# Values and gates of two heads, and the first merge branch, loaded in rows of 512 columns with halves that take turns

## The chip, the cores and the metric

One core of one Trainium2 chip runs the whole program: TensorE (PE, with its weight loads as PEld), VectorE (DVE), ScalarE (ACT), GpSimd (POOL), and SyncE (SP), which issues nearly all DMAs. The metric is the time of one execution on the device in microseconds; lower is better.

## The reference, cut to what matters

One layer of a hybrid decoder runs over 288 tokens (256 of a prompt, 8 samples of 4). All weights are read once, so the kernel is a long stream of matmuls against weights that pass through.

```python
D_MODEL = 2048; RET_HEADS = GLA_HEADS = 4; DV = 256; GDN_HEADS = 8
h = rmsnorm(x, norm_mix)
(rq, rk, rv, rg, dqkv, da, db, dz, lq, lk, lv, llr, lgt, mg) = split(h @ w_in)   # 16416 columns
y_ret = rmsnorm(retention(rq, rk, rv)) * silu(rg)             # 4 heads, value width 256
y_gdn = rmsnorm(gated_delta(conv(dqkv), ...)) * silu(dz)      # 8 heads
y_gla = rmsnorm(gla(lq, lk, lv, ...)) * silu(lgt)             # 4 heads, value width 256
gates = sigmoid(mg + b_merge)                                  # 3 branches x 2048 columns
x = x + (sum_i gates_i * (y_i @ w_branch[i])) @ w_o
x = x + (silu(hn @ w_gate) * (hn @ w_up)) @ w_down             # hn = rmsnorm(x)
```

## The kernel before

Every product is computed transposed: a block of 128 weight columns is the stationary operand, and the 288 tokens stream past it. Weights and activations are fp32. Each is split into a rounded part and a rest (`wh` and `wl`, `xh` and `xl`), and three matmuls (wh·xh, wh·xl, wl·xh) make one product of a 128 x 128 block. SP loads a weight piece `raw` of 512 KB, ACT casts it to `wh` (128 x 512 elements), DVE subtracts to get `wl`, PE multiplies. There are four buffers each of `raw`, `wh` and `wl`, and one `wh` with its `wl` feeds 12 matmuls.

The work comes in two shapes of load. In the mixers and in merge branch 0, `dense` and `products` (L361 to L401) take 256 columns: a `raw` is four k-tiles (4 x 128 rows of the weight) of 256 columns, so each row of it is 1 KB. I call a product of 256 columns over all 16 k-tiles a unit; it is four raws and 96 matmuls, and it accumulates in two of the four PSUM banks `pd`. In merge branches 1 and 2, the output projection and the feed-forward part, `wide` and `products4` (L326 to L359) take 512 columns: a `raw` is two k-tiles of 512 columns, 2 KB a row. These accumulate in four banks, turn by turn in `pd` and in `pm`.

The mixers run in the order gdn 0, ret 0, gdn 1, ret 1, gdn 2, gla 0, gdn 3, gla 1. A gdn pair has four units (q, k, v, gate). A ret or gla pair has six: q, k, and then value and gate of its first head, value and gate of its second. The mixing itself (scores, states, norms, on `pm`) is written as generators. `pump` (L158) advances them a step after each k-tile of a unit: one step for gdn mixing, then one for all other kinds. So mixing of one pair lies between the matmuls of the next units. A ret or gla head starts after its gate unit, as `ret_head` (L1084) or `gla_head` (L1157), and both end in `wide_head` (L943).

The gdn mixing inverts 8 x 8 blocks on DVE, and it moves them by way of DRAM: `bt` is written to `dgb` and `dgbs` (L684, L685), read back as `b8` (L688), solved in `u8` (L692 to L704), written to `dgu` and `dgus` (L706), and read as `uc` (L709). All these DMAs are issued on SP in one queue with the raws. L692 is the copy that sets `u8` up for the next gdn pair; it must wait until the writes out of the old `u8` have landed.

Merge branch 0 (`branch`, L1256) is eight times a gate unit (`mg`, 16 k-tiles) and a product with `w_branch` (8 k-tiles), both in 256 columns, while the last gla heads are still mixed. The order on each engine is made by the framework's scheduler, in which the weight loads, casts and subtractions have high priority.

Of the kernel before, what the change touches and what calls it, by code (L numbers as in the profile page):

```python
# [10 lines left out]
F32 = mybir.dt.float32  # L11
F32R = mybir.dt.float32r
I32 = mybir.dt.int32
AF = mybir.ActivationFunctionType
ALU = mybir.AluOpType
# [3 lines left out]
P = 128  # L19
# [5 lines left out]
T = NPR + NS  # L25
KT = D // P
# [4 lines left out]
WIDE = 512  # L31
CHUNK = 256
# [9 lines left out]
EV = 9  # L42

O_RQ, O_RK, O_RV, O_RG = 0, 512, 1024, 2048
O_GQ, O_GK, O_GV = 3072, 4096, 5120
O_DA, O_DZ = 6144, 6160
O_LQ, O_LK, O_LV, O_LLR, O_LG = 7184, 7696, 8208, 9232, 9248
O_MG = 10272
# [47 lines left out]
def blocks(t):  # L96
    return [t[:, k] for k in range(t.shape[1])]


class Trunk:  # L100
# [225 lines left out]
    def wide(self, xh, xl, wv, kt, evict):  # L326
# [5 lines left out]
            evict(m, tiles[m][:, :T])  # L332
        return pool

    def products4(self, xh, xl, wv, kt, steps=None):
        nc, tc = self.nc, self.tc
        pool, tag = ((self.pd, "pd"), (self.pm, "pm"))[self.turn]
        self.turn = 1 - self.turn
        acc = [self.t(pool, (P, 512), tag) for _ in range(4)]
        for k0 in range(0, kt, 2):  # L340
            raw = self.t(self.wp, (P, 2, WIDE), "raw", bufs=4)
            with tc.high_priority():
                nc.sync.dma_start(out=raw, in_=wv[:, k0:k0 + 2])
            for k in range(2):
                wh = self.t(self.wp, (P, WIDE), "wh", F32R, bufs=4)
                wl = self.t(self.wp, (P, WIDE), "wl", F32R, bufs=4)
                with tc.high_priority():
                    nc.scalar.copy(wh, raw[:, k])  # L348
                    self.tt(wl, raw[:, k], wh.bitcast(F32), ALU.subtract)
                kk = k0 + k  # L350
                for m in range(4):
                    ms = slice(m * P, (m + 1) * P)
                    o = acc[m][:, :T]
                    self.mm(o, wh[:, ms], xh[kk], kk == 0, False)
                    self.mm(o, wh[:, ms], xl[kk], False, False)
                    self.mm(o, wl[:, ms], xh[kk], False, kk == kt - 1)
            if steps is not None:
                next(steps)
        return (pool, tag), acc  # L359
# [208 lines left out]
    def gated(self, n, c0):  # L568

        out = self.t(self.mx, (P, 2, T), "ev", bufs=EV)  # L570

        def ev(m, pp):
            th = self.r1()
            self.tt(out[:, m], pp, self.rb, ALU.mult)
            self.act(th, out[:, m], AF.Tanh, scale=0.5)
            self.stt(out[:, m], th, 1.0, out[:, m], ALU.add, ALU.mult)

        self.x_in(c0, ev)
        return out

    def finish(self, tr_ps, gate, gcol, n, blk):

# [360 lines left out]
    def wide_head(self, h, st, st2, vt, vs, zq, kd, s0, state_out, p_out, decay, sg, gcols, n):  # L943


        nc, m = self.nc, self.wd
# [52 lines left out]
            nc.sync.dma_start(out=dst, in_=src)  # L999
        yield  # L1000
        yield
        for e in range(2):
            pt = self.ps()
            for g, (t0, w) in enumerate(GROUPS):
                self.tr(pt[:, t0:t0 + w], ys[g][:, e * P:(e + 1) * P])
            self.finish(pt, sg[:, e], None if gcols is None else gcols[:, e:e + 1], n, 2 * h + e)
        yield
        k3 = self.stack_k(kd[:NS, 2])
        v3 = self.stack_v(vs)
# [3 lines left out]
        for z in range(2):  # L1013
            for y in range(2):
# [5 lines left out]
                for b2 in range(2):  # L1020
                    b = 2 * y + b2
# [109 lines left out]
    def ret(self, pair):  # L1131
        q = self.rotated(O_RQ + pair * CHUNK)
        k = self.rotated(O_RK + pair * CHUNK)
        for hh in range(2):
            h = 2 * pair + hh
            v = self.evict_scaled(O_RV + h * 256)
            sg = self.gated(2, O_RG + h * 256)
            self.start(self.ret_head(h, q[:, hh], k[:, hh], v, sg), 1, "ret")


    def gla_logits(self, pair):
# [97 lines left out]
    def gla(self, pair):  # L1239
        b = self.t(self.mx, (P, 2, T), "ev", bufs=EV)  # L1240
        self.nc.sync.dma_start(out=b, in_=self.fsum[pair])
        q = self.t(self.mx, (P, 2, T), "ev", bufs=EV)

        def evq(m, pp):
            self.stt(q[:, m], pp, DK ** -0.5, self.rb, ALU.mult, ALU.mult)

        self.x_in(O_LQ + pair * CHUNK, evq)
        k = self.evict_scaled(O_LK + pair * CHUNK)
        for hh in range(2):
            h = 2 * pair + hh  # L1250
            v = self.evict_scaled(O_LV + h * 256)
            sg = self.gated(2, O_LG + h * 256)
            self.start(self.gla_head(h, q[:, hh], k[:, hh], v, sg, b[:, hh]), 1, "gla")


    def branch(self, n, order, emit=None):  # L1256
        nc = self.nc
        wb = self.i["w_branch"][0, n].rearrange("(k p) c -> p k c", p=P)
        yh, yl = [], []
        for k in range(8):  # L1260
# [4 lines left out]
            self.split(h, l, yr)  # L1265
            yh.append(h)
            yl.append(l)
        W = WIDE if n else CHUNK
        for j in range(D // W):
            th = [self.t(self.bp, (P, T), "bt", bufs=8) for _ in range(W // P)]  # L1270

            def evg(m, pp):
                blk = n * KT + W // P * j + m
                self.tt(th[m], pp, self.rb, ALU.mult)
                self.act(th[m], th[m], AF.Tanh, scale=0.5, bias=self.hbm[:, blk:blk + 1])

            if n:
                self.wide(blocks(self.xh), blocks(self.xl), self.w_in(O_MG + n * D + j * W, W), KT, evg)
            else:
                self.x_in(O_MG + j * W, evg)  # L1280

            def evb(m, pp):
                k = W // P * j + m
# [8 lines left out]
                    self.tt(self.acc[k], self.acc[k], th[m], ALU.add)  # L1292
                    emit(k, self.acc[k])

            (self.wide if n else self.dense)(yh, yl, wb[:, :, j * W:(j + 1) * W], 8, evb)

    def accs(self):
        return [self.t(self.ap, (P, T), "acc", bufs=KT) for _ in range(KT)]
# [193 lines left out]
```

## Time and profile before

| | |
|---|---|
| median of 3 runs | 2325.01 us (2323.74 to 2328.38) |
| profiled execution | 2326.31 us, of which the span from first to last instruction is 2324.2 us |
| granted TensorE clock, mean | 0.966 |
| PE busy | 2193.6 us (94%) |
| DVE busy, ACT busy | 1350.2 us (58%), 1027.2 us (44%) |
| DMA queue of SP | 366.22 MB, 64.4% of 16 engines' span |

The span falls into mixers (to about 866 us), merge branch 0 (866 to 1056 us) and the rest in rows of 512 columns. A busy share near 100% does not say that PE runs at its best, since a matmul's record is longer than the distance to the next one. Idle time, granted clock and matmuls per stretch say more. The granted clock is a share of 2.4 GHz and takes two levels, 1.0 and 0.5 (1.2 GHz); a value between is a mean over a stretch.

### The profile page before, as it was taken

What the parts mean: (1) busy time and instruction counts of PE and PEld (TensorE: products, weight loads), DVE (VectorE), ACT (ScalarE), POOL (GpSimd) and SP (SyncE); (2) the same over time, 40 slices, a digit from 0 to 9 for tenths busy, and PEclk for the clock granted to TensorE, in tenths of its full rate; (3) what the DMA queues carried; (4) which work ended last, traced back from release to release, by engine and by line L of the source; (5) the groups of instructions that cost most, each with busy time, mean ns of one, the idle gap of its engine ahead of it and who ended that gap; (6) DMA issues with size and microseconds to landing.
All of it is one profiled execution on the core that took longest, in us unless ns stands there. A gap on an engine that the chain in (4) does not pass through costs nothing.

```text
span 2324.2 us, 42820 instructions
## 1 busy us (share of the span) xinstructions
PE 2193.6 (94%) x16476; PEld 2131.1 (92%) x16476; DVE 1350.2 (58%) x2940; ACT 1027.2 (44%) x2114; POOL 209.5 (9%) x264
## 2 busy tenths in 40 slices
PE   8686998998699899999999999999999999999997
PEld 7686898988599898899999999999999999999997
DVE  4564676675378667455555655555555445555554
ACT  4352454454246445344444444444444334444443
POOL 2000230141024214100000000000000000000000
PEclk8897999998799999999999999999999999999999
DMA  8977576588766677877666656655555555555553
GB/s 172 110 113 116 138 179 148 122 185 137 108 149 158 160 127 190 175 188 203 174 180 181 166 173 193 181 167 164 166 169 165 165 167 169 164 165 168 167 157 121
DMA packets 287128, 371.73 MB, mean 160 GB/s; under 512 B 26242, under 2 KB 184028, under 8 KB 286764
## 3 DMA queue, kind: packets, MB, share of 16 engines
q1 hardware_dynamic: 285756, 366.22, 64.4%
q8 instruction: 129, 2.11, 0.4%
q0 software_dynamic: 896, 2.45, 0.3%
q14 instruction: 75, 0.61, 0.1%
q10 hardware_dynamic: 272, 0.34, 0.1%
HBM read 342.02 MB, written 26.92 MB: 159 GB/s over the span
## 4 chain that ended last, share of the span: by engine, by line
PE 80%; DMA 13%; DVE 3%; SPq 1%; ACT 1%; issue 1%; POOL 0%; POOLq 0%; DVEq 0%; ACTq 0%
PE pd L127 49%; PE pm L127 30%; DMA raw<-in_w_in_dram 5%; DMA dgu<-u 1%; PE pm L124 1%; DMA dgb<-bt 1%; DMA srow<-in_state_gdn_conv_dram 1%; DMA yr<-ys 1%; DVE wl L133 1%; DMA s<-in_state_ret_dram 1%; DMA out_dram<-s 1%; DMA uc<-dgu 1%; DMA b<-dgbs 1%; DMA ev<-fsum 0%; SPq L706 0%
## 5 line engine op out<-in xcount | busy, mean ns | idle before, releaser
L133 DVE TENSOR_TENSOR wl<-raw,wh 128x512 fp32r<-128x512 f32 (+1 forms) x1208 | 847.3, 705 | 738.8 <-ACT wh L348 490.9
L127 PE MATMUL pd<-xh,wh 128*128 128x288 f32 x2768 | 838.1, 304 | 37.5 <-ACT wh L384 33.1
L127 PE MATMUL pd<-xh,wl 128*128 128x288 f32 x2768 | 832.0, 304 | 34.0 <-DVE wl L133 33.9
L127 PE MATMUL pd<-xl,wh 128*128 128x288 f32 x2768 | 836.2, 303 | 0.2 <-DVE xl L142 0.2
L348 ACT CAST wh<-raw 128x512 fp32r<-128x512 f32 x784 | 485.0, 620 | 644.1 <-PE pd L127 331.7
L127 PEld LDWEIGHTS pd<-xh,wh 128*128 128x128 f32 x2768 | 535.0, 194 | 46.1 <-ACT wh L384 36.5
L127 PEld LDWEIGHTS pd<-xh,wl 128*128 128x128 f32 x2768 | 532.4, 194 | 42.1 <-DVE wl L133 38.5
L127 PEld LDWEIGHTS pd<-xl,wh 128*128 128x128 f32 x2768 | 535.6, 194 | 3.9 <-issue 1.0
L384 ACT CAST wh<-raw 128x512 fp32r<-128x512 f32 x416 | 254.6, 619 | 362.3 <-PE pd L127 234.8
L127 PE MATMUL pm<-xh,wl 128*128 128x288 f32 x704 | 207.8, 295 | 0.0
L127 PE MATMUL pm<-xl,wh 128*128 128x288 f32 x704 | 207.3, 294 | 0.0
L127 PE MATMUL pm<-xh,wh 128*128 128x288 f32 x704 | 207.0, 294 | 0.0
L127 PEld LDWEIGHTS pm<-xh,wl 128*128 128x128 f32 x704 | 132.1, 188 | 0.0
L127 PEld LDWEIGHTS pm<-xh,wh 128*128 128x128 f32 x704 | 132.1, 188 | 0.0
L127 PEld LDWEIGHTS pm<-xl,wh 128*128 128x128 f32 x704 | 132.0, 188 | 0.0
L127 PE MATMUL pd<-ah,wl 128*128 128x288 f32 x352 | 103.9, 295 | 0.0
L127 PE MATMUL pm<-ah,wl 128*128 128x288 f32 x352 | 103.9, 295 | 0.0
L127 PE MATMUL pm<-al,wh 128*128 128x288 f32 x352 | 103.8, 295 | 0.0
L127 PE MATMUL pd<-al,wh 128*128 128x288 f32 x352 | 103.7, 295 | 0.0
L127 PE MATMUL pm<-ah,wh 128*128 128x288 f32 x352 | 103.7, 295 | 0.0
L127 PE MATMUL pd<-ah,wh 128*128 128x288 f32 x352 | 103.6, 294 | 0.0
L147 POOL TENSOR_TENSOR fr<-fs,c_mh 128x3 f32<-128x3 f32 x1 | 0.8, 850 | 836.8 <-DVE fs L139 836.8
(367 smaller groups left out, 2894.8 us busy)
## 6 DMA issues: line engine op xcount, KB each, us to landing
raw<-in_w_in_dram SPq DMA_DIRECT2D x252, 512.0 KB
raw<-in_w_gate_up_dram SPq DMA_DIRECT2D x176, 512.0 KB
raw<-in_w_down_dram SPq DMA_DIRECT2D x88, 512.0 KB
raw<-in_w_branch_dram SPq DMA_DIRECT2D x48, 512.0 KB
raw<-in_w_o_dram SPq DMA_DIRECT2D x32, 512.0 KB
out_dram<-s SPq DMA_DIRECT2D x16, 512.0 KB
s<-in_state_gdn_dram SPq DMA_DIRECT2D x8, 512.0 KB
s<-in_state_ret_dram SPq DMA_DIRECT2D x16, 256.0 KB
```

The costliest lines, as they stand in the source:

```text
L124: self.nc.tensor.transpose(out, in_, self.ident[:k, :k])
L127: self.nc.tensor.matmul(out, lhsT=lhsT, rhs=rhs, start=start, stop=stop)
L133: self.nc.vector.tensor_tensor(out, a, b, op=op)
L147: self.nc.gpsimd.tensor_tensor(out, in_, c[:n].to_broadcast(list(in_.shape)), op=ALU.pow)
L348: nc.scalar.copy(wh, raw[:, k])
L384: nc.scalar.copy(h, src)
```

## The change

`halves` is a new product routine. It loads 512 columns in rows of 2 KB, as `wide` does: two raws of two k-tiles each, both needed for a group of four k-tiles. It then works through the group's left 256 columns and after that through its right 256, so that the halves take turns by four k-tiles. The left half accumulates in two `pd` banks and the right half in the other two, and the left half is evicted while the right one finishes. It pumps as `products` does.

`two_heads` uses it for ret and gla: one call for the values of both heads of a pair, then one for both gates. Head 0 starts after the values (before: after its value and its gate, the same number of units) and waits for its gate only near its end (`while not sg`). Head 1 starts after the gates. Merge branch 0 uses `halves` for gates and products, four times in 512 columns in place of eight times in 256. Units of gdn, and q and k of ret and gla, stay as they are.

```diff
+    def halves(self, xh, xl, wv, kt, evict):
+        acc = [self.t(self.pd, (P, 512), "pd") for _ in range(4)]
+        for k0 in range(0, kt, 4):
+            raws = []
+            for z in (k0, k0 + 2):
+                raw = self.t(self.wp, (P, 2, WIDE), "raw", bufs=4)
+                with tc.high_priority():
+                    nc.sync.dma_start(out=raw, in_=wv[:, z:z + 2])
+                raws.append(raw)
+            for half in range(2):
+                for z, raw in enumerate(raws):
+                    wh = self.t(self.wp, (P, 2, CHUNK), "wh", F32R, bufs=4)
+                    wl = self.t(self.wp, (P, 2, CHUNK), "wl", F32R, bufs=4)
+                    src = raw[:, :, half * CHUNK:(half + 1) * CHUNK]
+                    with tc.high_priority():
+                        nc.scalar.copy(wh, src)
+                        self.tt(wl, src, wh.bitcast(F32), ALU.subtract)
+                    for k in range(2):
+                        kk = k0 + 2 * z + k
...
+                        self.pump(k)
+                if k0 + 4 == kt:
+                    for m in range(2):
+                        evict(2 * half + m, acc[2 * half + m][:, :T])
...
+    def two_heads(self, cv, cg, head, kind):
+        vs = [self.t(self.mx, (P, 2, T), "ev", bufs=EV) for _ in range(2)]
...
+        self.x_halves(cv, evv)
+        gates = []
+        self.start(head(0, vs[0], gates), 1, kind)
+        gs = [self.t(self.mx, (P, 2, T), "ev", bufs=EV) for _ in range(2)]
...
+        self.x_halves(cg, evg)
+        gates.extend(gs)
+        self.start(head(1, vs[1], gates), 1, kind)
...
+        while not sg:
+            yield
...
-        for hh in range(2):
-            h = 2 * pair + hh
-            v = self.evict_scaled(O_RV + h * 256)
-            sg = self.gated(2, O_RG + h * 256)
-            self.start(self.ret_head(h, q[:, hh], k[:, hh], v, sg), 1, "ret")
+        self.two_heads(O_RV + pair * WIDE, O_RG + pair * WIDE,
+                       lambda hh, v, sg: self.ret_head(2 * pair + hh, q[:, hh], k[:, hh], v, sg), "ret")
...
-        W = WIDE if n else CHUNK
+        W = WIDE
...
-                self.x_in(O_MG + j * W, evg)
+                self.x_halves(O_MG + j * W, evg)
...
-            (self.wide if n else self.dense)(yh, yl, wb[:, :, j * W:(j + 1) * W], 8, evb)
+            (self.wide if n else self.halves)(yh, yl, wb[:, :, j * W:(j + 1) * W], 8, evb)
```

SP's queue, where ret 0 goes over from its k unit to the values, before. The rows from L684 on are the gdn mixing's way through DRAM.

```order
L323 DMA raw_328_1615<-in_w_in_dram 128x4x256
L323 DMA raw_348_1688<-in_w_in_dram 128x4x256
L1146 DMA r2_333_1635<-in_gla_w_up_dram 16x256
L1146 DMA r2_340_1664<-in_gla_w_up_dram 16x256
L323 DMA raw_366_1764<-in_w_in_dram 128x4x256
L323 DMA raw_371_1802<-in_w_in_dram 128x4x256
L684 DMA dgb_94_473<-bt4_282_1400 128x512
L685 DMA dgbs_95_474<-bt2_283_1401 32x64
L323 DMA raw_376_1836<-in_w_in_dram 128x4x256
L688 DMA b8_319_1551<-dgb_94_473 16x8x8 x4
L323 DMA raw_384_1876<-in_w_in_dram 128x4x256
L688 DMA b8_319_1551<-dgbs_95_474 4x8x8 x2
```

The same place in the changed kernel:

```order
L323 DMA raw_328_1615<-in_w_in_dram 128x4x256
L345 DMA raw_351_1691<-in_w_in_dram 128x2x512
L1204 DMA r2_333_1635<-in_gla_w_up_dram 16x256
L1204 DMA r2_340_1664<-in_gla_w_up_dram 16x256
L345 DMA raw_352_1693<-in_w_in_dram 128x2x512
L345 DMA raw_374_1805<-in_w_in_dram 128x2x512
L743 DMA dgb_94_473<-bt4_282_1400 128x512
L744 DMA dgbs_95_474<-bt2_283_1401 32x64
L345 DMA raw_375_1807<-in_w_in_dram 128x2x512
L747 DMA b8_319_1551<-dgb_94_473 16x8x8 x4
L747 DMA b8_319_1551<-dgbs_95_474 4x8x8 x2
L345 DMA raw_384_1874<-in_w_in_dram 128x2x512
```

From the fifth raw on, loads of 128x4x256 have become 128x2x512, the same bytes in half as many rows. The small DMAs keep their places, except that both reads of `dgbs` now stand ahead of the next raw.

DVE's queue a little later, at the end of ret 0's k unit, before. `r1<-pd` and `ev<-pd` evict the k unit's two banks, and `u8<-b8` waits for the reads on SP above:

```order
L133 TENSOR_TENSOR wl_365_1745<-raw_348_1688,wh_364_1744 128x512
L139 TENSOR_SCALAR ev_331_1633<-pm_335_1641,cols_85_441 128x288
L133 TENSOR_TENSOR wl_368_1767<-raw_366_1764,wh_367_1766 128x512
L133 TENSOR_TENSOR r1_343_1675<-pd_300_1469,rot_240_1191 64x288 x2
L133 TENSOR_TENSOR r1_344_1680<-pd_301_1470,rot_240_1191 64x288 x2
L693 COPY u8_320_1552<-b8_319_1551 72x4
L133 TENSOR_TENSOR wl_370_1787<-raw_366_1764,wh_369_1786 128x512
```

The same place in the changed kernel:

```order
L133 TENSOR_TENSOR wl_369_1750<-raw_352_1693,wh_368_1749 128x512
L139 TENSOR_SCALAR ev_331_1633<-pm_335_1641,cols_85_441 128x288
L133 TENSOR_TENSOR wl_371_1770<-raw_351_1691,wh_370_1769 128x512
L752 COPY u8_320_1552<-b8_319_1551 72x4
L133 TENSOR_TENSOR r1_343_1675<-pd_300_1469,rot_240_1191 64x288 x2
L133 TENSOR_TENSOR r1_344_1680<-pd_301_1470,rot_240_1191 64x288 x2
L133 TENSOR_TENSOR pr2_355_1707<-b8_319_1551,u8_320_1552 72x8
L133 TENSOR_TENSOR wl_373_1790<-raw_352_1693,wh_372_1789 128x512
```

The copy `u8<-b8` stands after the same number of `wl` subtractions, but now ahead of the evictions of the k unit, and the second `wl` already needs the second raw.

## Rows read from the trace of the kernel before

**Rows 1.** The page, part 2: the span in 40 slices of 58 us
```profile
PE   8686998998699899999999999999999999999997
...
PEclk8897999998799999999999999999999999999999
DMA  8977576588766677877666656655555555555553
```

**Rows 2.** Stretches, a late one: engines' busy us (instructions), granted clock, DMA share, GB/s
```profile
1300.00:1350.00 50.00, 50.00 (x380) 50.00 (x379) 27.73 (x50) 23.38 (x41) 0.00 (x0) 1.00 0.55 168
```

**Rows 3.** Stretches: ret 0 in two, ret 1's and gla's values and gates
```profile
134.00:184.00 50.00, 38.48 (x263) 34.43 (x262) 29.20 (x99) 26.27 (x68) 3.04 (x2) 0.93 0.74 114
184.00:261.00 77.00, 64.67 (x580) 60.85 (x579) 37.47 (x89) 24.01 (x51) 2.88 (x6) 0.87 0.65 118
...
384.00:454.50 70.50, 67.33 (x624) 63.60 (x623) 38.43 (x98) 26.54 (x61) 7.19 (x10) 0.98 0.59 123
...
577.00:673.00 96.00, 74.40 (x648) 69.67 (x647) 46.47 (x136) 28.06 (x66) 16.11 (x23) 0.86 0.65 110
...
788.00:866.00 78.00, 71.75 (x648) 66.68 (x647) 45.03 (x129) 28.13 (x64) 15.96 (x23) 0.98 0.69 122
```

**Rows 4.** Waits by engine, 168 to 184 us: in total, times, longest
```profile
DVE u L693 <- DMA b<-dgbs: 13.0, 1, 13.0
...
PE pd L127 <- DVE wl L133: 9.3, 1, 9.3
```

**Rows 5.** Waits by engine, 200 to 216 us
```profile
DVE u L692 <- DMA dgu<-u: 14.7, 1, 14.7
...
PE pd L127 <- DVE wl L133: 9.9, 1, 9.9
...
PE pd L127 <- ACT wh L384: 2.0, 1, 2.0
```

**Rows 6.** Waits by engine, 575 to 616 us
```profile
DVE u L693 <- DMA b<-dgbs: 13.5, 1, 13.5
...
PE pm L127 <- DVE tmc L718: 10.1, 1, 10.1
...
PE pd L127 <- DVE wl L133: 9.5, 1, 9.5
DVE u L692 <- DMA dgu<-u: 9.8, 1, 9.8
```

**Rows 7.** SP in order of time, 158 to 176 us: start, us until issued, line, DMA
```profile
160.72 0.34 SPq L684 DMA_DIRECT2D dgb<-bt  x1
...
172.67 1.75 SPq L688 DMA_DIRECT2D b<-dgb  x4
```

**Rows 8.** Stretches: while raws of 1 KB rows are loaded
```profile
216.00:234.00 18.00, 17.61 (x214) 16.59 (x214) 9.65 (x22) 6.33 (x10) 0.57 (x2) 0.84 0.53 130
...
566.00:578.00 12.00, 12.00 (x95) 11.84 (x94) 7.97 (x27) 4.29 (x10) 0.00 (x0) 1.00 0.99 88
```

**Rows 9.** DMA packets from 566 to 578 us
```profile
DMA packets 1046, 1.05 MB, mean 88 GB/s; under 512 B 32, under 2 KB 1045, under 8 KB 1045
```

**Rows 10.** Stretches: while raws of 2 KB rows are loaded (branch 1)
```profile
1121.00:1139.00 18.00, 18.00 (x138) 18.00 (x138) 11.06 (x20) 6.83 (x11) 0.00 (x0) 1.00 0.73 182
1158.00:1176.00 18.00, 18.00 (x138) 18.00 (x137) 10.76 (x20) 7.60 (x14) 0.00 (x0) 1.00 0.61 178
```

**Rows 11.** DVE in order of time, 168 to 184 us: the copy, [idle before it <- what ended that]
```profile
181.90 0.17 DVE L693 COPY u<-b 72x4 f32<-72x4 f32 x1 [12.97 <-DMA b<-dgbs]
```

**Rows 12.** PE's waits, 966 to 992 us; then the stretch
```profile
PE pd L127 <- ACT wh L384: 4.1, 2, 2.4
...
972.00:992.00 20.00, 15.54 (x89) 14.60 (x88) 7.92 (x14) 5.65 (x11) 0.00 (x0) 0.83 0.96 174
```

**Rows 13.** DVE in order of time, 364 to 386 us: an eviction of the k unit
```profile
366.74 0.92 DVE L133 TENSOR_TENSOR r<-pd,rot 64x288 f32<-64x288 f32 x2
...
369.92 0.46 DVE L133 TENSOR_TENSOR ev<-pd,rot 128x288 f32<-128x288 f32 x1
```

More of the change, by code (lines that the diff above doesn't have):

```diff
@@ L333, in wide, with x_halves @@
         return pool
+    def halves(self, xh, xl, wv, kt, evict):
+        nc, tc = self.nc, self.tc
+        acc = [self.t(self.pd, (P, 512), "pd") for _ in range(4)]
[17 more added lines that the diff above has]
+                        for m in range(2):
+                            ms = slice(m * P, (m + 1) * P)
+                            o = acc[2 * half + m][:, :T]
+                            self.mm(o, wh[:, k, ms], xh[kk], kk == 0, False)
+                            self.mm(o, wh[:, k, ms], xl[kk], False, False)
+                            self.mm(o, wl[:, k, ms], xh[kk], False, kk == kt - 1)
+                        self.pump(k)
+                if k0 + 4 == kt:
+                    for m in range(2):
+                        evict(2 * half + m, acc[2 * half + m][:, :T])
+    def x_halves(self, c0, evict):
+        self.halves(blocks(self.xh), blocks(self.xl), self.w_in(c0, WIDE), KT, evict)
     def products4(self, xh, xl, wv, kt, steps=None):
@@ L579, in gated, with evv, evg @@
         return out
+    def two_heads(self, cv, cg, head, kind):
+        vs = [self.t(self.mx, (P, 2, T), "ev", bufs=EV) for _ in range(2)]
+        def evv(m, pp):
+            self.tt(vs[m // 2][:, m % 2], pp, self.rb, ALU.mult)
+        self.x_halves(cv, evv)
+        gates = []
+        self.start(head(0, vs[0], gates), 1, kind)
+        gs = [self.t(self.mx, (P, 2, T), "ev", bufs=EV) for _ in range(2)]
+        def evg(m, pp):
+            out = gs[m // 2][:, m % 2]
+            th = self.r1()
+            self.tt(out, pp, self.rb, ALU.mult)
+            self.act(th, out, AF.Tanh, scale=0.5)
+            self.stt(out, th, 1.0, out, ALU.add, ALU.mult)
+        self.x_halves(cg, evg)
+        gates.extend(gs)
+        self.start(head(1, vs[1], gates), 1, kind)
     def finish(self, tr_ps, gate, gcol, n, blk):
@@ L1005, in wide_head @@
                 self.tr(pt[:, t0:t0 + w], ys[g][:, e * P:(e + 1) * P])
-            self.finish(pt, sg[:, e], None if gcols is None else gcols[:, e:e + 1], n, 2 * h + e)
+            self.finish(pt, sg[h % 2][:, e], None if gcols is None else gcols[:, e:e + 1], n, 2 * h + e)
         yield
@@ L1248, in gla @@
         k = self.evict_scaled(O_LK + pair * CHUNK)
[L1249 to L1253, printed above, removed]
+        self.two_heads(O_LV + pair * WIDE, O_LG + pair * WIDE,
+                       lambda hh, v, sg: self.gla_head(2 * pair + hh, q[:, hh], k[:, hh], v, sg, b[:, hh]), "gla")
     def branch(self, n, order, emit=None):
```

## The prediction

> **What bounds the kernel now.** I start on the page with the 40 slices [rows 1]: from the seventeenth slice on PE's digit is 9 nearly throughout. A late stretch shows what PE does when nothing is short: 380 matmuls in 50 us, 132 ns each, at clock 1.00 [rows 2]. A raw feeds 24 matmuls, so PE takes one raw (512 KB) in 24 x 0.132 = 3.16 us, and there the DMA engines are only 55% busy. The first 16 slices are different: 6 and 8 stand among PE's nines, 7 and 8 among PEclk's, and DMA's digits are mostly above the late ones. So I go to the stretches of the mixers [rows 3]. Second pairs lose little: ret 1 from its first value on is 70.5 us with 3.2 us of PE idle, gla 1 78 us with 6.3 us. First pairs lose much: ret 0 in 134 to 261 us has 11.5 + 12.3 = 23.8 us idle, and gla 0 21.6 us in the 96 us that hold the units gla 1 does in 78.
>
> The waits say why. At 168 to 184 us DVE stands 13.0 us in `u8<-b8`, until small blocks have come back from DRAM; `wl` is behind it on DVE, and PE idles 9.3 us [rows 4]. At 200 to 216 us DVE stands 14.7 us at L692, until the writes out of `u8` have landed, and PE idles 9.9 + 2.0 us [rows 5]. gla 0 has both again: 13.5 and 9.8 us on DVE, 9.5 and 10.1 us on PE [rows 6]. SP's timeline shows the first wait being made: `dgb<-bt` is issued at 160.72, and the read of what it wrote only at 172.67, 12 us for 256 KB, because several raws are queued ahead of it [rows 7]. So the bound in these places is the time that raws take in the DMA engines, and PE pays through small DMAs behind them.
>
> Why are raws slow there and not elsewhere? The stretches tell two kinds apart [rows 8]. At 566 to 578 us the engines are 0.99 busy and move only 88 GB/s; at 216 to 234 us the same 1 KB rows give 130 GB/s at 0.53, 2.8 times as much for their busy share. Counting raw issues along SP, four to a unit, the slow stretch holds the values of gla's head 0, the first unit that falls into its 1,024 columns of `w_in`; the quick one holds values and gates of ret's head 1, whose 1,024 columns head 0 has read from before. Along the trace it is so throughout: stretches like the first lie at the first unit of each 1,024 columns (ret 0's values and gates of head 0, gla 0's, and two gate units of branch 0 among them), and at no later one. The slow stretch shows 1046 packets in 12 us, 87 rows a us [rows 9]. At that rate a raw of 512 rows takes 5.9 us, twice what PE needs for it. Branch 1 reads first and second pieces of the same tensor in 2 KB rows: 0.73 and 0.61 busy at 182 and 178 GB/s, and PE is 18.00 of 18 us busy at clock 1.00 in both [rows 10]. 182 GB/s is 89 rows of 2 KB a us. I read this as: **the first pass over a stretch of columns goes by the row, at some 87 rows a us, whatever the row's length.**
>
> **The change part by part.** *Loads.* A raw of 2 KB rows has 256 rows: 256 / 87 = 2.9 us on a first pass, against 5.9 us. The loads of ret 0's and gla 0's values and gates, and of two of branch 0's four gate calls, are such passes. They now last eight raws, not four, but at half the time each, below PE's 3.16 us.
>
> *The `u8<-b8` wait* [rows 4, 7]. Order and place of its DMAs on SP are kept, and the raws ahead need half the time. `dgb<-bt` took 12 us; at half that its read starts about 167 us, before or as DVE gets there (its 12.97 us of idling ended at 181.90, so it began near 169 [rows 11]). The reads need a little longer, but PE then has the `wh` and `wl` in stock. Of 9.3 us I leave 1: -8.3.
>
> *The L692 wait* [rows 5]. Up to two raws of a first pass lie ahead of the last writes. I count what ret 1 keeps in its whole stretch of the same steps, 3.2 us [rows 3], as left over: 9.9 + 2.0 - 3.2 gives -8.7.
>
> *gla 0.* The same two steps; its stretch goes towards gla 1's: 21.6 - 6.3 = -15.3 [rows 3].
>
> *Branch 0.* At 972 to 992 us PE waits 4.1 us for casts while the DMA engines are 0.96 busy [rows 12]: -4.1. The rest of branch 0 has PE busy.
>
> *Clock.* After these gaps PE runs at the lower level. In 184 to 261 us the mean is 0.87, which is 0.13 x 77 / 0.5 = 20 us at 1.2 GHz; 12.3 us of the stretch are idle, so some 8 us of work ran at half speed and 4 us went. 577 to 673 us by the same sum: 27 - 21.6 = 5 us of work, 2.7 us. 972 to 992 us and the first part of ret 0, each a little: in all about 8 us, of which I take -7.
>
> *Second pairs* of ret and gla: raws were not short, the small DMAs land a little earlier: -1, between 0 and -9.5, their whole idle time [rows 3]. Sum of gains: 8.3 + 8.7 + 15.3 + 4.1 + 7 + 1 = **44.4 us**.
>
> *What it costs.* Casts, subtractions, matmuls and pumps keep number and size, and run beside PE as before; I cost them at nothing. New is that a call takes all four `pd` banks. The right half starts 24 matmuls (3.2 us) after the call before ended, and by then that call's last two banks must be evicted. For a k unit of ret that takes from 366.74 to 370.38, 3.6 us [rows 13], and the copy `u8<-b8` now stands ahead of it: some 0.4 us or more, twice; values, gates and branch 0 need one to two short DVE operations for a bank and fit. No row shows this wait. From below it is nothing (a gain is excluded, since it is only a wait more), from above about 2 us (that eviction plus two subtractions ahead of it) at each of 16 calls, 32 us; I take 3, near the lower end, since branch 1's calls of four banks show PE without a gap. Also new: two raws come free almost together, and the second must be there one cast later, so the reserve shrinks from six casts to five, from 9.5 to 7.9 us at 1.58 us each, against 2 x 2.9 us for the pair. Bounds 0 to 6 (half a us to one at each first-pass call); I take 3. Head 0's wait for its gate comes after more steps than the gate call pumps, so it costs nothing unless the head gets ahead; then only its end moves.
>
> Net 44.4 - 6 = 38. The profiled execution took 2326.31 us (span 2324.2 plus 2.1 around it), 1.3 us above the median: 2326.3 - 38 - 1.3 = **2287 us**.
>
> **The rivals.** *Half of it* (0.22). The waits end by the small DMAs' own landing, and a first pass at 2.9 us a raw with mixing traffic beside it is still nearly full. Then the first wait of each pair goes (9.3 + 9.5) with its clock, and the second stays: about 19, so 2306. For it: first passes now last twice as many raws, so the `u8` writes of ret 0 fall into one for certain.
>
> *Nothing* (0.09). What is slow is bytes, or something that only lies at the same time. The quick 1 KB stretch moves nearly as many bytes for its busy share as the 2 KB ones (130 GB/s at 0.53, 178 at 0.61 [rows 8, 10]). Then 2 KB rows change nothing: 2324. The Trainium skill (DMA: Bandwidth & Descriptors, Specifications) states this rule: rows of 512 B or more suffice for line rate. By it the sum would be near zero. The slow stretch with its 1 KB rows at 0.99 busy and 88 GB/s speaks against it here, the quick one at 130 GB/s for it.
>
> *All of it and more* (0.07). Second pairs lose their idle time too and the new costs are nothing: 44.4 + 8.5, so 2272 or a little less.
>
> *Slower* (0.07). The four banks: `u8<-b8` stands ahead of the evictions, both heads' evictions queue behind subtractions, and PE waits 2 us at each of 16 calls, 32 us, while only half of the gain comes: 2338. It decides from 1.2 us a call on if half the gain comes, 2.6 us a call if all of it does.
>
> **How the numbers follow.** My forecast has 0.55, and I predict its time, 2287. A measurement of this kernel can tell about 0.2% (4.7 us) from no change. Faster holds the forecast, the half and the larger gain: 0.84; same 0.09; slower 0.07. For the range I leave out the last two, 0.16. At the low end stand the larger gain with first q and k units also helped, 2264; at the high end the half gain with the costs at 6 us more, 2312.
>
> **What would show it.** In the trace of the changed kernel: ret 0 from its k unit on without DVE waits above 5 us at `u8`; stretches of first passes in 2 KB rows near 170 GB/s, not 88; gla 0's values and gates in about 80 us, not 96; PEclk digits of 9 in these slices; branch 0 about 6 us shorter. Wrong would be the row rule, if first passes of 2 KB rows still moved 88 GB/s; the place of the wait, if raws are quick and DVE stands at `u8` as long; and the cost, if PE waits for `pd` evictions at the starts of calls.

## The result and the profile after

The changed kernel takes 2271.9 us (2265.5 to 2273.6), the kernel before 2324.4 us (2322.1 to 2328.4) on the same chip: a ratio of 0.9765, with a 95% interval of 0.9745 to 0.9784. It is 52 us faster. The prediction was 2287 us, 38 us less than the median before, with a range from 2264 to 2312. The profiled execution took 2270.85 us, with a span of 2269.0 us, 55.2 us less than before.

The page's 40 slices, which answer to [rows 1], come first:

```profile
PE   8699998998999999999999999999999999999997
...
PEclk8799999998999999999999999999999999999999
DMA  9876675587567555766666556655555555555553
```

From the third slice on two 8s stand among PE's nines, where before there were two 6s and four 8s. The next rows are stretches of the changed kernel, cut at the same matmuls as those of [rows 3], so that each holds the same work (columns as in [rows 2]): ret 0 in two, gdn 1, ret 1, gla 0 from its values on, gla 1 from its values on, branch 0, and the first 1,087 matmuls of branch 1.

```profile
134.40:176.10 41.70, 38.10 (x264) 33.92 (x262) 31.72 (x106) 25.76 (x68) 3.04 (x2) 1.00 0.72 146
176.10:241.20 65.10, 61.51 (x581) 58.12 (x580) 34.80 (x81) 24.44 (x51) 2.91 (x6) 0.97 0.60 134
241.20:368.60 127.40, 113.67 (x790) 105.49 (x790) 96.14 (x267) 63.13 (x169) 35.27 (x37) 0.95 0.68 164
368.60:434.50 65.90, 65.90 (x625) 62.21 (x625) 39.15 (x98) 26.80 (x62) 7.17 (x10) 1.00 0.49 136
...
556.50:631.70 75.20, 71.27 (x646) 66.43 (x645) 42.25 (x122) 27.58 (x64) 14.33 (x21) 0.98 0.57 118
...
745.60:815.00 69.40, 68.59 (x642) 64.45 (x641) 42.76 (x115) 27.94 (x64) 13.40 (x20) 1.00 0.42 123
815.00:997.20 182.20, 179.95 (x1343) 174.05 (x1342) 116.32 (x241) 89.26 (x193) 31.03 (x42) 1.00 0.68 195
997.20:1144.50 147.30, 144.60 (x1087) 143.88 (x1086) 78.97 (x137) 64.80 (x112) 0.00 (x0) 1.00 0.67 185
```

Set against the same stretches of before, the time went like this:

| stretch | before, us | after, us | difference |
|---|---|---|---|
| ret 0, first part | 50.0 | 41.7 | -8.3 |
| ret 0, second part | 77.0 | 65.1 | -11.9 |
| gdn 1 and what follows up to ret 1's first value | 123.0 | 127.4 | +4.4 |
| ret 1 from its values on | 70.5 | 65.9 | -4.6 |
| gla 0 from its values on | 96.0 | 75.2 | -20.8 |
| gla 1 from its values on | 78.0 | 69.4 | -8.6 |
| branch 0 | 190.0 | 182.2 | -7.8 |
| start of branch 1 | 144.0 | 147.3 | +3.3 |

These make -54.3 us of the 55.2; the rest is spread over what lies between. Each figure comes from one trace of each kernel, and two of the stretches vary by 5 us and more between traces, as the experiments show (ret 0's second part and gdn 1). ret 1 now has no PE idle time at all: 65.90 of 65.90 us, at clock 1.00.

The two waits of ret 0 answer to [rows 4] and [rows 5]. The first two rows below are from 160 to 185 us, the last two from 185 to 215 us of the changed kernel, waits by engine (in total, times, longest):

```profile
DVE u L752 <- DMA b<-dgbs: 3.0, 1, 3.0
...
PE pd L127 <- DVE ev L133: 1.3, 1, 1.3
```

```profile
PE pm L127 <- DVE tmc L777: 3.1, 1, 3.1
...
DVE u L751 <- DMA dgu<-u: 1.9, 1, 1.9
```

DVE's 13.0 us in `u8<-b8` are 3.0 us, and its 14.7 us ahead of setting `u8` up are 1.9 us. PE's 1.3 us behind `ev`, an eviction into which a call of four banks runs, are the only wait of this kind above 0.2 us up to the end of branch 0.

### The profile page after: what moved, and what is told of

It reads as the page before. It is cut to its first block, busy times and chain, and to the rows that moved or that the text cites. A ratio compares the mean times of both kernels' runs of the same rounds, so it can differ in the third digit from the quotient of the medians.

```text
span 2269.0 us, 42856 instructions
## 1 busy us (share of the span) xinstructions
PE 2178.8 (96%) x16476; PEld 2117.5 (93%) x16476; DVE 1356.2 (60%) x2940; ACT 1026.6 (45%) x2114; POOL 204.9 (9%) x264
## 4 chain that ended last, share of the span: by engine, by line
PE 79%; DMA 11%; DVE 4%; ACT 2%; SPq 1%; issue 1%; POOL 1%; POOLq 0%; DVEq 0%; ACTq 0%
PE pd L127 48%; PE pm L127 30%; DMA raw<-in_w_in_dram 4%; DMA yr<-ys 2%; DVE wl L133 1%; DMA s<-in_state_ret_dram 1%; PE pm L124 1%; DMA srow<-in_state_gdn_conv_dram 1%; DMA out_dram<-s 1%; DMA dgu<-u 1%; DVE r L142 1%; DMA uc<-dgu 0%; DMA ys<-yo 0%; SPq L202 0%; ACT wh L420 0%
## 5 line engine op out<-in xcount | busy, mean ns | idle before, releaser
L127 PEld LDWEIGHTS pd<-xh,wh 128*128 128x128 f32 x2768 | 529.6, 192 | 29.3 <-ACT wh L420 15.8
L127 PEld LDWEIGHTS pd<-xh,wl 128*128 128x128 f32 x2768 | 527.0, 192 | 8.5 <-DVE wl L133 5.6
```

The source lines that it names most:

```text
L127: self.nc.tensor.matmul(out, lhsT=lhsT, rhs=rhs, start=start, stop=stop)
```

## The experiments

The theory at this point: the first pass over 1,024 columns of `w_in` goes by the row, at some 87 rows a us, and the change gives PE twice the work for each such row. One rival is that the gain comes from the order of the work (head 0 starting before its gate, halves taking turns), not from the loads. Each run below was timed beside the kernel before; its ratio stands beside its time.

### The parts one by one

`pair0_only` and `pair1_only` use the new calls in the first, or in the second, pairs of ret and gla only; `branch_only` in merge branch 0 only.

```diff
-        self.two_heads(O_RV + pair * WIDE, O_RG + pair * WIDE, ...)
+        if pair == 0:                    # pair1_only: pair == 1; branch_only: never
+            self.two_heads(O_RV + pair * WIDE, O_RG + pair * WIDE, ...)
+        else:
+            ...                          # value and gate of one head after the other, as before
```

> Only the first pairs (ret 0 and gla 0) load values and gates as the changed kernel does; second pairs and branch 0 are as before. If first passes over columns go by the row and that is the gain (rows), the first pairs bring what the two traces differ by there: 8.3 + 11.9 us in ret 0 and 20.8 us in gla 0, less the 4.4 us that gdn 1 loses behind ret 0, so about 2324 - 37 = 2287 us; the two stretches of the second pairs stay at 70 and 78 us. If the gain comes from the order of the mixing (head 0 starting before its gate), first and second pairs would gain alike in share, some 25 us here: 2299 us. If the loss in gdn 1 isn't of this part, 2283 us.

> Only the second pairs (ret 1 and gla 1) load in rows of 512 columns with halves that take turns; first pairs and branch 0 are as before. By rows alone (second passes are quick anyway) hardly a gain: 2323 us, as the prediction had it. If a raw of half as many rows is shorter for what queues behind it, on quick passes too, the gain is what the traces differ by in these stretches, 4.6 + 8.6 us: 2311 us, and the two stretches take about 66 and 69.5 us without PE idle. If those gains come only because first pairs run earlier or tidier, nothing: 2324 us.

> Only merge branch 0 (gates and products) loads in rows of 512 columns with turns; the mixers are as before. From the traces: 7.8 us shorter in branch 0 and 3.2 us given back at the start of branch 1 makes 2324 - 4.6 = 2319 us, if both belong to this part. If the 3.2 us at the start of branch 1 are due to the mixers' tail, 2316 us. If the first passes of two of the gate calls were hidden anyway, 2324 us.

Measured: first pairs alone 2297.8 us (0.988, 0.9855 to 0.9904), second pairs alone 2320.5 us (0.998, 0.9968 to 0.9995), branch 0 alone 2315.4 us (0.997, 0.9953 to 0.9984), against 2324.1 us before. Their gains are 26.3, 3.6 and 8.7 us.

By its time the run of the first pairs missed what the theory expected (2287 us) and met the rival's 2299 us. But by the rival first and second pairs gain alike in share, and second pairs gained 3.6 us. And the stretches of the first pairs did gain what was expected: ret 0 takes 41.3 + 65.7 us and gla 0 75.9 us, as in the changed kernel. What is missing went elsewhere: gdn 1 is 4.7 us longer, as in the changed kernel, the work from behind ret 1 to gla 0's values 3.9 us (126.4 against 122.5), the start of branch 1 2.0 us. Second pairs, in the same stretches as above with gdn 2's first part between them, in `pair1_only`:

```profile
379.40:446.30 66.90, 65.86 (x625) 62.18 (x624) 37.73 (x92) 25.81 (x57) 6.39 (x9) 1.00 0.50 135
446.30:515.30 69.00, 63.74 (x447) 59.48 (x447) 52.23 (x135) 34.51 (x90) 27.31 (x29) 0.98 0.76 171
781.30:855.80 74.50, 70.62 (x642) 66.02 (x642) 43.28 (x119) 27.18 (x63) 14.54 (x20) 0.98 0.53 115
```

ret 1 gains 3.6 us and gla 1 3.5 us, well above the prediction's 1 us together, and gdn 2 gives 5.5 us back (63.5 us before). What gives it back stands in that stretch's waits:

```profile
ACT sh L1011 <- DMA s<-in_state_ret_dram: 8.5, 1, 8.5
...
PE pm L127 <- ACT sh L1011: 5.3, 1, 5.3
```

ACT's casts `sh` wait for the states of ret's heads, and PE for the casts. One reading is that the states do not arrive earlier when a ret pair ends earlier. It is not shown: in `pair0_only` ret 1 loads as before and takes 71.2 us, and the casts still wait 6.8 us for states behind it.

Branch 0 alone takes 179.7 us, 10.3 us less, and branch 1 behind it 149.1 us, 5.1 us more. The start of branch 1 also takes 2.0 and 1.6 us more in `pair0_only` and `pair1_only`, whose branch 0 is that of before; so a part of that loss does not come from branch 0; how much is not settled.

The three gains make 38.6 us, the whole change brings 52. A stall of about 5 us stands in gdn 2 in some of these traces and not in others (in `pair0_only` and `pair1_only`, not in the changed kernel), and ret 0's second part took 72 us and not 77 in the traces of `pair1_only` and `branch_only`, which have there the same work as before. Where such a stall falls is not settled by what was changed in that place; that the sum falls short is shown, its exact cause stays open.

### Long rows, or half the passes?

`split_rows` is the changed kernel with each raw loaded by two DMAs of 256 columns, so that its rows are 1 KB again; order, casts and matmuls stay.

```diff
-                    nc.sync.dma_start(out=raw, in_=wv[:, z:z + 2])
+                    for c in (0, CHUNK):
+                        nc.sync.dma_start(out=raw[:, :, c:c + CHUNK], in_=wv[:, z:z + 2, c:c + CHUNK])
```

> The changed kernel, but every raw of the new routine is loaded by two DMAs of 256 columns (1 KB rows), left and then right; nothing else moves. If what costs is the first pass over a stretch of columns (rows), only the left DMA pays: 256 rows at 87 rows/us are 2.9 us, the right one is quick, about 1.2 us, 4.1 us a raw where PE needs 3.2: some 5 us lost at each of four first-pass calls and little elsewhere, about 2290 us. If rows of 1 KB are slow in such stretches as such, a raw takes 5.9 us, 22 us lost a call in four to six calls: 2350 us or more. If the gain came from order and banks, no difference: 2272 us.

Measured: 2278.7 us (0.980, 0.9781 to 0.9819). About 45 of the 52 us are there with rows of 1 KB. That is 11 us faster than the theory expected, which had the left half of each raw still at 87 rows a us, and 7 us from the 2272 us expected if only order and banks mattered. The stretch of ret 0's values, 160 to 172 us, in the changed kernel and in `split_rows`, and under it the packets of the latter:

```profile
160.00:172.00 12.00, 12.00 (x77) 10.40 (x77) 8.10 (x25) 7.58 (x14) 0.00 (x0) 1.00 0.75 167
```

```profile
160.00:172.00 12.00, 12.00 (x77) 10.24 (x76) 8.61 (x27) 7.58 (x15) 0.00 (x0) 1.00 0.68 156
```

```profile
DMA packets 2463, 1.87 MB, mean 156 GB/s; under 512 B 808, under 2 KB 2334, under 8 KB 2462
```

2334 - 808 = 1526 packets of 512 B to 2 KB, which are the 1 KB rows, in 12 us are 127 rows a us. The engines were busy for 0.68 of the time, so 1 KB rows went at 187 a us of busy time or more, since other packets took part of it. So rows of 1 KB are not slow as such. Nor does the theory's sum fit. By [rows 8] and [rows 9] slow rows go at some 85 a us of busy time; the quick ones moved 130 GB/s at 0.53, some 240 rows a us. Half of each, one behind the other, would make some 125 a us, an estimate from these rows. By the 187, columns which are slow when loaded alone lose most of their slowness when the 256 columns beside them are loaded at the same time. It is no matter of these 12 us alone: from 152 to 215 us, which hold the loads of ret 0's values and gates, `split_rows` moves 137 GB/s at 0.66, 208 GB/s of busy time, where half of each would give some 130. Why, no run shows.

The Trainium skill (Perfetto Trace Analysis, DMA Optimizations) says that DMAs under 2 KB carry a significant overhead each and that larger ones pay. Each load of a raw here is a DMA of 256 or 512 KB, so this bears on the case only if it is read of rows. Read so, this case shows little of it: by busy time the two stretches move 156 / 0.68 = 229 and 167 / 0.75 = 223 GB/s, and the step from 1 KB to 2 KB rows, with half as many DMAs, is worth 7 or 8 us of the 52 (by the times, or by the ratios). The rest does not hang on the row's length.

### Is it the first read?

If a first read is dear, a cheap read ahead of it should help. `touch_gla` is the kernel before, with small reads of 16 bytes of each row of gla's value and gate columns, some 140 to 240 us ahead of use (in head 1's columns, so that nothing head 0 needs is read); `touch_ret` reads in columns that have been read before; `after_touch_q` is the changed kernel with small reads of gla's query columns.

```diff
+                t = self.t(self.mx, (P, 4, 4), "touch", bufs=8)
...
+                    self.nc.scalar.copy(t[:, 0, 0:1], raw[:, 0, 0:1])
+                    self.nc.scalar.dma_start(out=t, in_=self.w_in(c, 4)[:, 4 * q:4 * q + 4])
...
+                self.touch = [(c, q) for c in (O_LV + 256, O_LG + 256) for q in range(4)]
```

> The kernel before, with eight small reads added on ACT's queue, between some 385 and 510 us: of all 2048 rows, 16 bytes each, in the 1,024 columns of gla's values and in those of its gates (at the columns of head 1, so that nothing head 0 needs is read). Nothing reads what they bring. If the first read of a row in such a stretch of columns is what is dear, whatever its length, and later ones are quick, then gla 0's values and gates are quick now: its stretch goes from 96 us to about 78 as gla 1's, and the whole to about 2309 us, with 0 to 5 us lost where the small reads run. If a first pass is slow for another reason (its place in the program, what else is under way), 2324 us or a few more and gla 0 stays at 96 us.

> The same eight small reads at the same places, but in the columns of ret's values and gates, which have been read long before. If only first reads are dear, these are quick and change nothing: gla 0 stays at 96 us and the whole at 2324 us. If eight more DMAs on another queue change the timing by themselves, it shows here.

> The changed kernel, with four small reads of gla's query and key columns (2048 rows, 16 bytes each) added on ACT's queue during ret 1. gla 0's query unit is the one first pass between 140 us and branch 0 that the change left in rows of 1 KB; in the stretch that holds it PE idles 7.3 us and 13.7 us run at the lower clock. If the first read is what is dear, that goes and the whole is 2262 to 2266 us. If not, 2272 us, or up to 5 more for the traffic.

Measured: `touch_gla` 2330.5 us (1.002, 1.0005 to 1.0031), `touch_ret` 2332.1 us (1.003, 1.0009 to 1.0041), `after_touch_q` 2275.2 us (0.978, 0.9767 to 0.9796, against 0.9765 without the reads). None helped. The first row is from `touch_gla` while gla 0's first values are loaded, the second the packets of 374 to 375.6 us, when one small read runs:

```profile
572.00:584.00 12.00, 12.00 (x93) 11.84 (x94) 8.28 (x23) 4.61 (x11) 1.17 (x2) 1.00 1.01 83
```

```profile
DMA packets 528, 0.01 MB, mean 5 GB/s; under 512 B 528, under 2 KB 528, under 8 KB 528
```

512 rows were touched in 1.6 us, and the values were as slow afterwards as before (88 GB/s at 0.99 in [rows 8]). gla 0 took 95.3 us. The half of the theory that says "first", in the sense of the first read of a row among these 1,024 columns, did not survive this.

### First, or certain columns?

In the kernel before, the slow units are always the first to read their 1,024 columns, and they are also always the first 256 of them (ret's and gla's queries and keys count as 1,024 together). By the offsets at L44 to L48 these 256 all begin 0 to 32 columns behind a multiple of 1,024 of `w_in`. `other_order` parts the two: the kernel before with head 1 ahead of head 0, and branch 0's blocks in the order 3, 2, 1, 0, 7, 6, 5, 4. `pairs_swapped` is the changed kernel with pair 1 ahead of pair 0.

```diff
-        for hh in range(2):
+        for hh in (1, 0):
...
-        for f, pair in ((self.gdn, 0), (self.ret, 0), (self.gdn, 1), (self.ret, 1),
-                        (self.gdn, 2), (self.gla, 0), (self.gdn, 3), (self.gla, 1)):
+        for f, pair in ((self.gdn, 1), (self.ret, 1), (self.gdn, 0), (self.ret, 0),
+                        (self.gdn, 2), (self.gla, 1), (self.gdn, 3), (self.gla, 0)):
```

> The kernel before, with another order of the same loads in rows of 1 KB: in each ret and gla pair head 1's value and gate come ahead of head 0's, and branch 0 goes through its eight blocks of 256 columns as 3, 2, 1, 0, 7, 6, 5, 4. If the first pass over 1,024 columns is slow (as the prediction reads it), the slow units are now head 1's value and gate, and branch 0's blocks 3 and 7: slow stretches at the same times as before, 160 to 202 us, 566 to 609 us, and about 2325 us. If certain columns are slow whenever they are read (the first 256 of each 1,024: head 0's, and blocks 0 and 4), the slow stretches move behind by a value and a gate unit (ret: to about 190 to 225 us; gla: to 600 to 640 us), and in branch 0 to blocks 0 and 4, fourth and eighth in turn. The time then depends on what waits there: 2315 to 2330 us.

> The changed kernel, with the order of pairs gdn 1, ret 1, gdn 0, ret 0, gdn 2, gla 1, gdn 3, gla 0, in place of 0, 0, 1, 1, 2, 0, 3, 1; the work of each pair is the same. If a first pass is slow, whichever columns come first, nothing changes: slow stretches at 79 to 141 us and about 2272 us. If certain columns are slow (the first 256 of each 1,024, which only first pairs read), the units of gdn 1 and ret 1 at the start of the program are quick, 79 to 141 us shrink by up to 3 x 6 + 5 us, and what gdn 0 loses later is less, since there PE has mixing to do between: 2250 to 2268 us.

Measured: `other_order` 2309.1 us (0.994, 0.9923 to 0.9957), `pairs_swapped` 2249.7 us (0.9685, 0.9668 to 0.9703). Three stretches of `other_order`, with head 1's value first, then head 0's value and gate, and the packets of the second:

```profile
160.00:172.00 12.00, 12.00 (x77) 10.24 (x77) 9.17 (x26) 7.59 (x14) 0.00 (x0) 1.00 0.81 143
198.00:210.00 12.00, 2.07 (x8) 1.49 (x7) 1.40 (x3) 1.14 (x2) 0.00 (x0) 0.71 0.96 90
222.00:234.00 12.00, 12.00 (x164) 11.26 (x163) 6.54 (x15) 4.23 (x8) 0.56 (x2) 1.00 0.99 85
```

```profile
DMA packets 1420, 1.08 MB, mean 90 GB/s; under 512 B 330, under 2 KB 1420, under 8 KB 1420
```

Head 1's value, now the first to read these columns, is quick: 143 GB/s at 0.81. Head 0's value and gate are slow, 90 and 85 GB/s with the engines full, although head 1 has read next to them; 1420 - 330 = 1090 packets of 512 B or more in 12 us are at most 91 rows a us. In branch 0 of `other_order` the engines are full at 82 GB/s in 925 to 935 us and at 78 GB/s in 1012 to 1022 us, in the fourth and the eighth block in turn, which are the blocks 0 and 4. And the start of the program, 79 to 141 us, in the kernel before and in `pairs_swapped`, with the stretch of the latter in which gdn 0's query comes under it:

```profile
79.00:141.00 62.00, 46.54 (x284) 44.09 (x283) 33.57 (x87) 24.10 (x50) 3.83 (x4) 0.84 0.93 98
```

```profile
79.00:141.00 62.00, 62.00 (x455) 58.75 (x454) 51.43 (x152) 39.11 (x91) 2.65 (x2) 1.00 0.61 158
174.00:186.00 12.00, 12.00 (x97) 11.07 (x96) 5.15 (x16) 5.17 (x15) 1.30 (x3) 1.00 0.98 84
```

With pair 1 first, nothing is slow there: PE is busy for all of the 62 us. The slow stretch comes when gdn 0 is loaded, third in turn. **Certain columns are slow, in whatever order they are read**, when they are loaded by themselves: the first 256 of each 1,024 of a kind. Both runs say so. In `pairs_swapped` PE stays busy for 12.00 of 12 us while the slow load runs later, with mixing to do between the matmuls. `other_order` pays there: in its second stretch PE is busy for 2.07 of 12 us. It gains where quick columns now come first, in ret 0's first part (43.9 us, 50.0 before) and in gla 0 (82.6 us, 96.0 before), and loses some of it in branch 0.

### Do the halves have to take turns?

`no_turns` keeps the loads of 512 columns, but casts and multiplies each k-tile over its whole width, and evicts all four banks at the end of a call.

```diff
-            for half in range(2):
-                for z, raw in enumerate(raws):
...
+            for k in range(2):
...
+                    nc.scalar.copy(wh, raw[:, k])
...
+                for m in range(4):
```

> The changed kernel, but in the calls on 512 columns of w_in and w_branch the halves don't take turns: each k-tile is cast and multiplied in all its 512 columns, as branches 1 and 2 do, and all four banks are evicted at the end of the call. The loads are the same. If the loads are the gain and the turns only spare the evictions, the bounds are 2272 us and 2272 + 16 calls x 2 us = 2304 us; I expect 2280. If the turns make the gain, it is lost: 2315 us or more. If the turns cost something (two raws at once, banks in pairs), 2265 us.

Measured: 2270.1 us (0.976, 0.9743 to 0.9772), the same as with turns. The turns neither cost nor bring anything that could be told here. That leaves head 0's start before its gate, which no run changed by itself. In ret 0's first part, before any head of ret starts, the 8.3 us are there without it. So is `branch_only`'s gain in branch 0, which starts no heads. And `other_order` gains 6.1 us in that first part and 13.4 us in gla 0 with the old routine and the old start, by other columns alone. In ret 0's second part it is argued that the loads are the gain, from DVE's waits and from the same number of units ahead of each head.

### What was given back, and a faster version

`four_states` gives the heads' states a fourth buffer, at the cost of two small working buffers of one kind and one of another. `pairs_spread` changes the order of pairs once more, so that the two slow pairs of the start do not follow each other.

```diff
-R1 = 4
-R2 = 6
+R1 = 3
+R2 = 4
...
-            s = self.t(self.mx, (P, 1024), "s0", bufs=3).rearrange("p (b e) -> p b e", e=256)
+            s = self.t(self.mx, (P, 1024), "s0", bufs=4).rearrange("p (b e) -> p b e", e=256)
```

```diff
+        for f, pair in ((self.gdn, 1), (self.ret, 1), (self.gdn, 0), (self.gla, 1),
+                        (self.gdn, 2), (self.ret, 0), (self.gdn, 3), (self.gla, 0)):
```

> The changed kernel, with four buffers for the heads' states in place of three; the room is taken from two small working buffers (two of six of one kind, one of four of the other). The change lost 4.4 us in gdn 1, where PE waits for ACT's casts of ret's states, and these for the states' loads, which need a free buffer. If the buffers hold them up, that comes back: PE idles some 5 us less in gdn 1, and the whole is 2264 to 2268 us. If the loads' own time does, or the smaller working buffers cost as much, 2270 to 2278 us.

> The changed kernel, with the order of pairs gdn 1, ret 1, gdn 0, gla 1, gdn 2, ret 0, gdn 3, gla 0, so that no pair that reads slow columns (the pairs numbered 0) stands behind another. In the run with gdn 0 and ret 0 one behind the other these two pairs held most of the idle time that PE had left, 15.7 and 12.9 us. If certain columns are slow and their transfers can be spread under mixing, up to 10 us of that go: 2238 to 2248 us. If what idles there is mixing's own chain (states that arrive late), 2250 us or a few more.

Measured: `four_states` 2269.2 us (0.976, 0.9728 to 0.9794), `pairs_spread` 2249.8 us (0.968, 0.9647 to 0.971). Waits in gdn 1's stretch, in the changed kernel and then in `four_states`:

```profile
ACT sh L1011 <- DMA s<-in_state_ret_dram: 15.9, 2, 9.0
...
PE pm L127 <- ACT sh L1011: 5.7, 2, 4.2
```

```profile
ACT sh L1011 <- DMA s<-in_state_ret_dram: 9.3, 2, 6.9
...
PE pm L127 <- ACT sh L1011: 1.5, 1, 1.5
```

PE's wait is 4.2 us shorter, and gdn 1 goes from 127.4 to 124.2 us. This is one trace of each, and the stretch moves by more than that without such a change: in `no_turns`, with the same loads and three buffers, it takes 120.0 us, 3.0 less than before. So that the buffer is what helps is not shown by the stretch. The whole gains less than its interval can tell from none. For `pairs_spread` the second expectation came true: the order is no better than `pairs_swapped`, and around 228 us PE stands 8.1 us for the casts of states. `pairs_swapped` and `pairs_spread` are the fastest versions here, about 20 us below the changed kernel (22 by the times, 19 by the ratios).

## Why the prediction was right, and where it was not

*Which loads are slow.* The step that failed is the sentence "the first pass over a stretch of columns goes by the row, at some 87 rows a us, whatever the row's length". `other_order` and `pairs_swapped` show that it is the columns and not the pass. In the kernel before the two coincide in every unit, and so the rows chosen could not tell them apart. "Whatever the row's length" fails too. The 89 rows of 2 KB a us were read where the engines were 0.73 busy and PE was never short [rows 10]; that is near the rate at which PE takes them (a raw in 3.16 us is 81 a us), and no limit of the engines. In the changed kernel ret 0's values move 167 GB/s at 0.75, which is some 109 rows of 2 KB a us of busy time.

The sum was not harmed, because it needed only that a raw takes less than PE's 3.16 us: at 167 / 0.75 = 223 GB/s of busy time 512 KB take some 2.35 us, where 2.9 were forecast and 5.9 were read before. The forecast of these terms thus came out by a wrong rule. What the rule would have harmed is the next change, since by the pass swapping pairs would bring nothing, and it brings about 20 us.

*The `u8<-b8` wait*: -8.3 was predicted, and the stretch is 8.3 us shorter. DVE's wait is 3.0 us in place of 13.0.

*The L692 wait*: -8.7, with some 4 us of clock beside it. The stretch is 11.9 us shorter, and 3.1 us of waiting are left on PE, as was allowed for (3.2). Some of this agreement is luck: in the traces of `pair1_only` and `branch_only`, with the same work there, the stretch took 72 us and not 77, and from those the gain is about 7.

*gla 0*: -15.3 and 2.7 of clock, 18 in all; measured 20.8. It came to 75.2 us, below the 78 that gla 1 had.

*Branch 0*: 4.1 us and a little clock, "about 6 us shorter"; measured 7.8, of which 3.3 go again at the start of branch 1, which was not foreseen. `branch_only` has 10.3 and 5.1.

*Second pairs*: this is the term that was mis-sized, at -1 (between 0 and -9.5), and it measured -4.6 and -8.6, 13 us. In `pair1_only` the two are -3.6 and -3.5, so about 7 of the 13 come with the new calls in second pairs alone; where the rest comes from stays open. I took small DMAs there to be held up by little, since raws were quick. The wait that DVE has for the writes out of `u8` stood in ret 1 too. It is shown first for the kernel before, then for the changed one and for `split_rows`, and last for `pair0_only`, where ret 1 loads as before:

```profile
DVE u L692 <- DMA dgus<-u: 5.6, 1, 5.6
```

```profile
DVE u L751 <- DMA dgus<-u: 1.6, 1, 1.6
```

```profile
DVE u L752 <- DMA dgus<-u: 2.3, 1, 2.3
```

```profile
DVE u L751 <- DMA dgus<-u: 5.6, 1, 5.6
```

It goes with the new call in that pair (`pair1_only` has 2.0 us of it), and with rows of 1 KB as well, so neither row length nor the first pair brings it. SP's order of time names what is different ahead of those writes, in the kernel before and in the changed one:

```profile
388.30 7.38 SPq L323 DMA_DIRECT2D raw<-in_w_in_dram  x3
395.99 2.75 SPq L706 DMA_DIRECT2D dgu<-u  x4
```

```profile
373.57 1.72 SPq L345 DMA_DIRECT2D raw<-in_w_in_dram  x2
377.98 1.27 SPq L765 DMA_DIRECT2D dgu<-u  x3
```

Three raws stood ahead of the writes, now two, and the queue has 2.7 us to empty before they come. This is read from the traces and was not tried by itself. The upper bound of -9.5 was the idle time of both stretches; the clock that goes with idle time was left out of it (0.98 in both stretches before, 1.00 after).

*Costs*: 6 us, of which 3 for the four banks and 3 for the reserve of casts. Of the first the trace shows 1.3 us, and `no_turns`, which evicts four banks at once, costs nothing that can be told; of the second nothing. In their place stand costs that the prediction did not have: gdn 1 is 4.4 us longer and the start of branch 1 3.3. That these come near 6 us is luck. In gdn 1 PE's waits for the casts of ret's states are 5.7 us and were 3.6 before; another, behind an eviction on DVE, is 6.5 us and was 1.1:

```profile
PE pm L124 <- DVE ev L142: 6.5, 1, 6.5
```

```profile
PE pm L124 <- DVE ev L142: 1.1, 1, 1.1
```

The first row is from the changed kernel, the second from the kernel before. What sets them off stays open.

The rival "all of it and more" gave 2272, which is the time measured, but by no costs at all and second pairs without idle time. The second half of that holds for ret 1 and nearly for gla 1; the first is right for the banks and wrong for the states. The rival "nothing", beside which the prediction named the Trainium skill (DMA: Bandwidth & Descriptors, Specifications: rows of 512 B or more suffice for line rate), has its share too. `split_rows` moves 1 KB rows at 187 or more a us of busy time; what the rule does not foresee is the stretches of slow columns alone, at 78 to 90 GB/s with the engines full.

## What to carry to other kernels

When one kind of load is slow, test both readings before building on one: that it comes first, and that it is that data; swapping the order of two equal pieces of work tells them apart in one run. A rate that was read while the DMA engines were not full need not be a limit. Where part of a tensor reads slowly by itself, load it together with parts that read quickly, or at a time when the compute engine has other work, so that the time of a load stays below what PE needs. In a queue that large loads and small dependent DMAs share, the small ones can wait for the large ones even where these are never late.

## What the runs showed of the hardware

In `w_in` (2048 rows of 16,416 fp32 columns), loads that held nothing but the first 256 of each 1,024 columns of a kind moved 78 to 90 GB/s with the DMA engines 0.96 to 1.04 busy, in whatever order. The same loads of other columns moved 130 to 143 GB/s at 0.53 to 0.81 busy. The stretches of `other_order` and `pairs_swapped` above are the two sides of it; here are ret 1 and gla 1 before, whose heads read the third and fourth quarters:

```profile
412.00:428.00 16.00, 16.00 (x202) 15.14 (x198) 9.42 (x20) 6.35 (x13) 0.57 (x2) 1.00 0.69 137
...
822.00:836.00 14.00, 14.00 (x161) 13.22 (x161) 8.29 (x18) 6.01 (x13) 0.74 (x2) 1.00 0.75 137
```

Loaded side by side with the next 256 columns, the slow ones no longer fill the engines: 156 GB/s at 0.68 in 1 KB rows, 167 GB/s at 0.75 in 2 KB rows. Reads of 16 bytes a row took 1.6 us for 512 rows, in columns of the second quarter, and did not help the reads that followed; in the slow columns none was tried. Why these columns are slow, and why company helps them, no run shows.
